# RWKV-7 layer on one Trainium2 core: squares for the norms summed on GpSimd, per-head sums issued in fours, low-rank second products on 128 rows

## The chip, the cores and the metric

The kernel runs on one core of one Trainium2 chip. A core has TensorE (PE, the matrix engine, which reads its stationary operand into the array and streams the other one through), VectorE (DVE), ScalarE (ACT), GpSimd (POOL) and SyncE (SP, which here only issues transfers). Each engine works through its own list of instructions in order; a semaphore makes one wait for another. The metric is the device time of one execution in microseconds, as the median of several runs.

## The reference

One layer (DEPTH is 1) on 2048 tokens of width 1024 in fp32, and a final norm:

```python
h = x
hn = rms_norm(h, norm_mix_g[i])
h = h + rwkv7_time_mix(hn, ...)
h = h + sq_relu_mlp(rms_norm(h, norm_ffn_g[i]), mlp_up[i], mlp_down[i])
return rms_norm(h, final_g)
```

Inside the time mix, what this case touches is

```python
w_log = -softplus(-(w0 + tanh(xw @ w1) @ w2)) - 0.5
a  = sigmoid(a0 + (xa @ a1) @ a2)            # w1, a1: 1024 x 64; w2, a2: 64 x 1024
kk = heads(k * k_k); kk = kk / max(norm(kk, axis=-1), 1e-12)
bonus = sum(r_h * k_h * r_k, axis=-1) * v_h  # 16 heads of 64
```

together with a recurrence over the tokens, a gate, and the output product. The MLP is `relu(x @ up)**2 @ down` with 4096 hidden columns.

## The kernel before, in words

Everything lies with the model's width on the partitions and tokens along the row: a tensor of a block is eight tiles of 128 rows by 512 tokens, and there are four blocks (NB). A product of fp32 operands is done on float32r tiles: each operand is split into a high part (a cast on ACT, L84 and L97) and the rest (a subtraction on DVE, L85 and L98), and `mm3` issues three matmuls of 512 columns (L90, L91, L92). Weights come by DMA (`wload`), 256 KB at a time.

**Phase A**, to about 690 us, does the projections of a block: `head(i)` loads the tokens and normalises them (norms a0 to a3), `lora(i)` does the first halves of the low-rank products, then `k_proj`, `r_proj` and `v_proj`. Beside the projections of a block runs `epilogue(i)` of the block before it, emitted in pieces after each eighth of `r_proj(i)` and `k_proj(i+1)`: reciprocal norms of the keys of each head, the second low-rank products into `pz` and `pq` (L388 and L389, L397 and L398), the decays, and what the recurrence reads (`ar`, `bk`), which goes to DRAM by DMAs issued on POOL's queue (L435, L436). `head(i+1)` and `lora(i+1)` are emitted within `r_proj(i)`.

**The low-rank second product.** `TW` holds the high part of `tanh(xw @ w1)` in rows 0 to 63 and the rest of it in rows 64 to 127; the weight's high part is loaded twice, in both halves of the rows. So L388 with 128 rows gives high times high plus high times rest. L389 adds the weight's low part times the high part of `TW`, with 64 rows. L397 and L398 do the same for `TA`, whose high part is in rows 64 to 127.

**Sums over a head.** In `k_proj` the square of each of the eight key tiles (`sq`, on ACT) is multiplied by a matrix with 32 columns (`selk`) into a strip of 32 rows of `psN`; tile m goes to strip m mod 4, and the two passes over the strips add up (L360). In `epilogue` the product `rk` = r times r_k times k (DVE, L431) goes the same way into `psO` (L433). One such matmul has 128 rows, 32 columns and 512 tokens, and each is issued when its row of data is ready. There are 8 in each of the 8 sums. In the trace a matmul of this kind, being fp32, leaves two records.

**norm(h)** (L105 to L127) is called 12 times: a0 to a3 in phase A, n0 to n3 before the MLP and f0 to f3 at the end of each block. ACT squares a tile (L110), and a matmul with 32 columns of ones (L112) adds up its partitions into strip k mod 4 of `pss`, again eight times. ACT copies `pss` out (L115); four matmuls with one column each (L118) sum the partitions once more into a column for each token (the ones are 1/32 there, because every strip holds 32 equal rows); DVE and ACT make the reciprocal root (L120 to L122), and four matmuls (L125) spread it over the 128 partitions. What follows waits for that: the normalised tiles of the next stage, or the output.

**Phase B** (about 690 to 1100 us) is the recurrence of the first block with products of other blocks as fillers. **Phase C** (to the end) does for each block the output product `c_out`, the norm `c_norm` (n), the MLP in groups (`c_up`, `c_down`) and the last norm `c_final` (f), with the recurrence of the next block in between. The order of the program is: last group of `c_down` first half, `c_out(i+1)`, `c_norm(i+1)`, `c_down` second half, `c_final(i)`, `c_up` of block i+1. `c_norm` keeps its spread reciprocal in a tile of the tag "rb", which has one buffer, and `c_final` takes the same buffer.

**The order of the work** on each engine is set when the program is built: a scheduler works from the emitted instructions, their dependences and buffers, and writes a fixed list for each engine. So an instruction may stand earlier or later than the place at which it was emitted.

**POOL** has almost nothing to compute: in phases B and C one select for each window (L574, 96 rows of 1024), and the issue of transfers (L293, L435, L436, L821).

Of the kernel before, what the change touches and what calls it, by code (L numbers as in the profile page):

```python
# [39 lines left out]
def trunk(ctx: ExitStack, tc, xt, vecs, lnw, lnb, wr, wk, wv, w1a1, w2, a2,  # L40
# [47 lines left out]
    def mm3(out, lhs, rhs, first, last):  # L88
        """out += lhs^T rhs for operands given as (high, low) pairs."""
        nc.tensor.matmul(out, lhs[0], rhs[0], start=first, stop=False)  # L90
        nc.tensor.matmul(out, lhs[0], rhs[1], start=False, stop=False)  # L91
        nc.tensor.matmul(out, lhs[1], rhs[0], start=False, stop=last)  # L92
# [12 lines left out]
    def norm(h, name, sb, ps, tag, tb, nb=1):  # L105
        """Reciprocal root mean square of each column of h, on all partitions."""
        pss = ps.tile([P, TB], F32, tag=tag, name=f"{name}s", bufs=nb)
        for k in range(KT):
            sq = sb.tile([P, TB], F32, tag="t0", name=f"{name}q{k}", bufs=tb)
            nc.scalar.activation(sq, h[k], AF.Square)  # L110
            j = k % 4
            nc.tensor.matmul(pss[32 * j:32 * j + 32], ones32[:, 0:32], sq, start=(k < 4), stop=(k >= 4),  # L112
                             skip_group_check=True, tile_position=(0, 32 * j))
        s = sb.tile([P, TB], F32, tag="t0", name=f"{name}c", bufs=tb)
        nc.scalar.copy(s, pss)  # L115
# [820 lines left out]
```

## Time and profile before

| what | value |
|---|---|
| median of three runs | 3051.98 us (3050.55 to 3055.19) |
| span of the profiled execution | 3052.7 us |
| PE busy | 2921.5 us, 96% of the span |
| DVE busy | 2029.8 us, 66% |
| ACT busy | 1450.6 us, 48% |
| POOL busy | 199.9 us, 7% |
| instructions | 50234 |

The profiled execution is 0.7 us longer than the median. Busy time is the time in which an engine had at least one instruction in work. A matmul of 512 columns shows about 0.39 us, but the next one begins 0.227 us after it, since matmuls overlap in the array: so what a matmul costs is read from the distance of the starts, and not from its duration. A view of windows gives, for a stretch of time, the busy time of each engine with its count of records. A view of groups gives, after the shape and the count, the busy time and the mean of one in nanoseconds, and after the bar the idle time before them and what ended it.

### The profile page before, as it was taken

What the parts mean: (1) busy time and instruction counts of PE and PEld (TensorE: products, weight loads), DVE (VectorE), ACT (ScalarE), POOL (GpSimd) and SP (SyncE); (2) the same over time, 40 slices, a digit from 0 to 9 for tenths busy, and PEclk for the clock granted to TensorE, in tenths of its full rate; (3) what the DMA queues carried; (4) which work ended last, traced back from release to release, by engine and by line L of the source; (5) the groups of instructions that cost most, each with busy time, mean ns of one, the idle gap of its engine ahead of it and who ended that gap; (6) DMA issues with size and microseconds to landing.
All of it is one profiled execution on the core that took longest, in us unless ns stands there. A gap on an engine that the chain in (4) does not pass through costs nothing.

```text
span 3052.7 us, 50234 instructions
## 1 busy us (share of the span) xinstructions
PE 2921.5 (96%) x19304; PEld 2126.9 (70%) x19304; DVE 2029.8 (66%) x3858; ACT 1450.6 (48%) x2649; POOL 199.9 (7%) x278
## 2 busy tenths in 40 slices
PE   7999999997899999999999999999999999999998
PEld 4756565655455577777776777777777777778886
DVE  4576767794788577676667678765866786454443
ACT  4556666663356344444444444443445435343442
POOL 0000000013021100000000000000000000000000
PEclk9999999998899999999999999999999999999999
DMA  3434444346564423333252333334233232332332
GB/s 120 147 135 154 146 155 146 130 172 214 162 179 160 155 88 112 113 97 111 89 159 87 108 94 111 112 100 150 90 111 107 92 117 87 104 118 94 96 100 76
DMA packets 192544, 373.94 MB, mean 122 GB/s; under 512 B 41136, under 2 KB 41712, under 8 KB 187696
## 3 DMA queue, kind: packets, MB, share of 16 engines
q1 hardware_dynamic: 175216, 305.49, 32.9%
q0 software_dynamic: 17088, 65.24, 5.5%
q8 instruction: 152, 2.49, 0.3%
q14 instruction: 88, 0.72, 0.1%
HBM read 303.32 MB, written 67.32 MB: 121 GB/s over the span
## 4 chain that ended last, share of the span: by engine, by line
PE 74%; DVE 13%; DMA 4%; ACT 4%; issue 3%; POOL 0%; SPq 0%; DVEq 0%; ACTq 0%; POOLq 0%
PE pd L92 7%; PE pd L90 6%; PE pd L91 6%; PE pu L90 6%; PE pu L91 6%; PE pu L92 6%; PE pv L176 2%; DVE tmp L580 2%; DVE M L581 2%; PE pr L92 2%; PE pr L90 2%; PE pk L90 2%; PE pk L91 2%; PE pr L91 2%; PE pk L92 2%
## 5 line engine op out<-in xcount | busy, mean ns | idle before, releaser
L92 PE MATMUL pd<-uh,d_wl 128*128 128x512 f32 x1024 | 408.7, 399 | 5.5 <-DVE d_wl L85 5.2
L90 PE MATMUL pd<-uh,d_wh 128*128 128x512 f32 x1024 | 407.3, 398 | 0.0
L91 PE MATMUL pd<-ul,d_wh 128*128 128x512 f32 x1024 | 404.3, 395 | 0.0
L84 ACT CAST d_wh<-d_w 128x512 fp32r<-128x512 f32 x256 | 158.5, 621 | 354.2 <-PE pu L91 157.9
L84 ACT CAST u_wh<-u_w 128x512 fp32r<-128x512 f32 x256 | 158.0, 621 | 312.1 <-PE pd L91 114.1
L812 DVE TENSOR_TENSOR h<-h,pd 128x512 f32<-128x512 f32 x256 | 174.2, 682 | 169.0 <-PE pd L92 168.2
L85 DVE TENSOR_TENSOR d_wl<-d_w,d_wh 128x512 fp32r<-128x512 f32 x256 | 180.6, 709 | 120.1 <-ACT d_wh L84 110.2
L85 DVE TENSOR_TENSOR u_wl<-u_w,u_wh 128x512 fp32r<-128x512 f32 x256 | 175.9, 693 | 90.1 <-ACT u_wh L84 73.1
L92 PEld LDWEIGHTS pd<-uh,d_wl 128*128 128x128 f32 x1024 | 193.0, 189 | 59.4 <-DVE d_wl L85 15.8
L91 PEld LDWEIGHTS pd<-ul,d_wh 128*128 128x128 f32 x1024 | 193.3, 189 | 46.6 <-issue 4.2
L90 PEld LDWEIGHTS pd<-uh,d_wh 128*128 128x128 f32 x1024 | 193.6, 189 | 44.2 <-issue 4.2
L580 DVE TENSOR_TENSOR tmp<-M 96x30 f32<-96x30 f32 (+14 forms) x480 | 156.2, 325 | 18.6 <-POOL M L574 8.1
L581 DVE TENSOR_TENSOR M<-M,tmp 96x30 f32<-96x30 f32 (+14 forms) x480 | 156.5, 326 | 11.1
L801 DVE TENSOR_TENSOR ul<-rl,uh 128x512 fp32r<-128x512 f32 x128 | 87.9, 687 | 65.8 <-ACT uh L800 65.6
L176 PE MATMUL pv<-v,xv 128*128 128x512 f32 x256 | 125.2, 625 | 5.9 <-DMA v<-in_wv 5.6
L562 PEld LDWEIGHTS sc<-Le,Bk 128*64 128x64 f32 x1024 | 66.3, 139 | 46.6 <-issue 33.2
L562 PE MATMUL sc<-Le,Bk 128*64 128x64 f32 x1024 | 76.9, 227 | 15.0 <-DMA Le<-d_ar 5.3
L634 PEld LDWEIGHTS pS<-suv,ls 128*64 128x64 f32 x1024 | 65.1, 137 | 34.4 <-ACT suv L631 26.5
L627 PEld LDWEIGHTS pu<-ws,xbd 128*128 128x128 f32 x512 | 65.1, 193 | 30.7 <-ACT xbd L594 16.5
L797 ACT ACTIVATE rl<-rl 128x512 f32<-128x512 f32 x128 | 80.9, 632 | 3.7
L634 PE MATMUL pS<-suv,ls 128*64 128x64 f32 x1024 | 75.0, 225 | 7.4 <-ACT suv L631 6.1
L627 PE MATMUL pu<-ws,xbd 128*128 128x64 f32 x512 | 67.5, 275 | 15.3 <-ACT xbd L594 9.2
(704 smaller groups left out, 7174.1 us busy)
## 6 DMA issues: line engine op xcount, KB each, us to landing
u_w<-in_up SPq DMA_DIRECT2D x256, 256.0 KB, 2.7
d_w<-in_down SPq DMA_DIRECT2D x256, 256.0 KB, 2.6
k_w<-in_wk SPq DMA_DIRECT2D x64, 256.0 KB, 2.6
r_w<-in_wr SPq DMA_DIRECT2D x64, 256.0 KB, 2.7
d_ar<-ar POOLq DMA_DIRECT2D x32, 512.0 KB, 3.2
d_bk<-bk POOLq DMA_DIRECT2D x32, 512.0 KB, 3.2
Bk<-d_bk SPq DMA_DIRECT2D x16, 1024.0 KB, 4.9
o_w<-in_wo SPq DMA_DIRECT2D x64, 256.0 KB, 2.9
```

The lines of the kernel that those rows point to most:

```text
L84: nc.scalar.copy(hi[0:rows, 0:cols], raw[0:rows, 0:cols])
L85: nc.vector.tensor_tensor(lo[0:rows, 0:cols], raw[0:rows, 0:cols], hi[0:rows, 0:cols], ALU.subtract)
L90: nc.tensor.matmul(out, lhs[0], rhs[0], start=first, stop=False)
L91: nc.tensor.matmul(out, lhs[0], rhs[1], start=False, stop=False)
L92: nc.tensor.matmul(out, lhs[1], rhs[0], start=False, stop=last)
L176: nc.tensor.matmul(pv[tt], xs_[k][:, c], w, start=(k == 0), stop=(k == KT - 1))
L562: nc.tensor.matmul(sc[64:128, p, :], bk[:, p, c, :], Le[:, p, c, :], start=(p == 0), stop=True, skip_group_check=True)
L580: nc.vector.tensor_tensor(tv, M[0:96, s + 1:32, s:s + 1].to_broadcast((96, n, s)), M[0:96, s:s + 1, 0:s].to_broadcast((96, n, s)), ALU.mult)
L581: nc.vector.tensor_tensor(M[0:96, s + 1:32, 0:s], M[0:96, s + 1:32, 0:s], tv, ALU.add)
L627: nc.tensor.matmul(pu[:, k, :], xbd[:, k, c, :], ws[:, k, :], start=(k == 0), stop=True, skip_group_check=True)
L634: nc.tensor.matmul(pS[0:64, p, :], lsc[0][:, p, :], S[0][:, p, :], start=(p == 0), stop=True, skip_group_check=True)
L812: nc.vector.tensor_add(h[m], h[m], pd)
```

## The change

The change has three parts. Comments are taken out as well, so line numbers move.

1. `norm` sums the squares on GpSimd. ACT's first square goes into a tile `s`, and each of the seven others is added to it by a GpSimd `tensor_tensor` (L124 of the changed kernel). The four matmuls that sum the partitions (L128 there) now read `s` and a column of 1.0. The matmuls of L112 and the copy of L115 go for ten of the twelve norms; with `late=True` (a0 and f3) the old way stays. `s` has one buffer: the tag "rb" in phase C, so the same as the spread reciprocals of `c_norm` and `c_final`, and "nsum" in phase A.
2. `headsum` issues the four matmuls of four tiles together, after the fourth; `sq` gets four buffers instead of two, and `rk` is written over `rr[m]`.
3. The second low-rank products take all 128 rows of the weight's low part (L405 and L414 there). This also adds the product of the low part and the rest.

```diff
+    def norm(h, name, sb, ps, tag, tb, nb=1, late=False, stag="rb"):
+        s = sb.tile([P, TB], F32, tag=stag, name=f"{name}c", bufs=1)
+        if late:
+            pss = ps.tile([P, TB], F32, tag=tag, name=f"{name}s", bufs=nb)
...
+            nc.scalar.copy(s, pss)
+            one = ones32[:, 32:33]
+        else:
+            nc.scalar.activation(s, h[0], AF.Square)
+            for k in range(1, KT):
+                sq = sb.tile([P, TB], F32, tag="t0", name=f"{name}q{k}", bufs=tb)
+                nc.scalar.activation(sq, h[k], AF.Square)
+                nc.gpsimd.tensor_tensor(s, s, sq, ALU.add)
+            one = ones32[:, 0:1]
...
-        psB = norm(xs, f"a{i}", am, psm, "mm", e.tb, e.mm)
+        psB = norm(xs, f"a{i}", am, psm, "mm", e.tb, e.mm, i == 0, "nsum")
...
+    def headsum(ps_, rows, half_):
+        for j in range(4):
+            nc.tensor.matmul(ps_[32 * j:32 * j + 32], selk[:, half_, :], rows[4 * half_ + j], start=(half_ == 0), stop=(half_ == 1),
+                             skip_group_check=True, tile_position=(0, 32 * j))
...
-            sq = ae.tile([P, TB], F32, tag="sq", name=f"sq{i}_{m}", bufs=2)
-            nc.scalar.activation(sq, pm, AF.Square, scale=vec[:, V_KK, m:m + 1])
-            j = m % 4
-            nc.tensor.matmul(psN[32 * j:32 * j + 32], selk[:, m // 4, :], sq, start=(m < 4), stop=(m >= 4),
+            sqs.append(ae.tile([P, TB], F32, tag="sq", name=f"sq{i}_{m}", bufs=4))
+            nc.scalar.activation(sqs[m], pm, AF.Square, scale=vec[:, V_KK, m:m + 1])
+            if m % 4 == 3:
+                headsum(psN, sqs, m // 4)
...
-                nc.tensor.matmul(pz, w2p[1][0:64, c], TW[0:64], start=False, stop=True)
+                nc.tensor.matmul(pz, w2p[1][:, c], TW, start=False, stop=True)
...
-                nc.tensor.matmul(pq, a2p[1][64:128, c], TA[64:128], start=False, stop=True)
+                nc.tensor.matmul(pq, a2p[1][:, c], TA, start=False, stop=True)
...
-                rk = ae.tile([P, TB], F32, tag="km", name=f"rk{i}_{m}", bufs=2)
-                nc.vector.scalar_tensor_tensor(rk, rr[m], vec[:, V_RK, m:m + 1], km, ALU.mult, ALU.mult)
-                j = m % 4
-                nc.tensor.matmul(psO[32 * j:32 * j + 32], selk[:, m // 4, :], rk, start=(m < 4), stop=(m >= 4),
+                nc.vector.scalar_tensor_tensor(rr[m], rr[m], vec[:, V_RK, m:m + 1], km, ALU.mult, ALU.mult)
+                if mm == 3:
+                    headsum(psO, rr, hf)
...
-        pb = norm(h, f"f{i}", cp, psb, "y0", 2)
+        pb = norm(h, f"f{i}", cp, psb, "y0", 2, 1, i == NB - 1)
```

What stands where on the engines, at three places. The names are those of the tiles (output, then inputs), with the number of the tile behind.

**PE behind the last output product of block 3 (norm n3), before.** `po3_7` is the last tile of that product, `n3q` are the squares, `pd2_7_4` is the first product of the second half of `c_down`.

```order
L92 MATMUL po3_7_24850<-z3_7h_24571,o3_7_1_wl_24872 128x512
L112 MATMUL n3s_24889<-n3q0_24890,ones32_100 32x512
L112 MATMUL n3s_24889<-n3q1_24893,ones32_100 32x512
L90 MATMUL pd2_7_4_25004<-uh2_28_23832,d2_7_0_1_wh_24982 128x512
L91 MATMUL pd2_7_4_25004<-ul2_28_23833,d2_7_0_1_wh_24982 128x512
L92 MATMUL pd2_7_4_25004<-uh2_28_23832,d2_7_0_1_wl_24983 128x512
L90 MATMUL pd2_7_4_25004<-uh2_29_24227,d2_7_1_1_wh_24988 128x512
L112 MATMUL n3s_24889<-n3q2_24896,ones32_100 32x512
L91 MATMUL pd2_7_4_25004<-ul2_29_24228,d2_7_1_1_wh_24988 128x512
L92 MATMUL pd2_7_4_25004<-uh2_29_24227,d2_7_1_1_wl_24989 128x512
L112 MATMUL n3s_24889<-n3q3_24899,ones32_100 32x512
L90 MATMUL pd2_7_4_25004<-uh2_30_24389,d2_7_2_1_wh_24994 128x512
```

And the same place in the changed kernel, where `n3c` is the sum that GpSimd makes:

```order
L92 MATMUL po3_7_24786<-z3_7h_24507,o3_7_1_wl_24808 128x512
L90 MATMUL pd2_7_4_24936<-uh2_28_23768,d2_7_0_1_wh_24914 128x512
L91 MATMUL pd2_7_4_24936<-ul2_28_23769,d2_7_0_1_wh_24914 128x512
L92 MATMUL pd2_7_4_24936<-uh2_28_23768,d2_7_0_1_wl_24915 128x512
L90 MATMUL pd2_7_4_24936<-uh2_29_24163,d2_7_1_1_wh_24920 128x512
L91 MATMUL pd2_7_4_24936<-ul2_29_24164,d2_7_1_1_wh_24920 128x512
L92 MATMUL pd2_7_4_24936<-uh2_29_24163,d2_7_1_1_wl_24921 128x512
L90 MATMUL pd2_7_4_24936<-uh2_30_24325,d2_7_2_1_wh_24926 128x512
L91 MATMUL pd2_7_4_24936<-ul2_30_24326,d2_7_2_1_wh_24926 128x512
L92 MATMUL pd2_7_4_24936<-uh2_30_24325,d2_7_2_1_wl_24927 128x512
L128 MATMUL n3t_24848<-ones32_100,n3c_24825 128x1 x4
L90 MATMUL pd2_7_4_24936<-uh2_31_24395,d2_7_3_1_wh_24932 128x512
```

The six places with L112 matmuls between the products are gone (two, one and one of them show above), and the four one-column matmuls that need the whole sum stand nine matmuls behind the last output product.

**PE in `k_proj` of block 2, changed kernel.** `sq2_0` to `sq2_3` are the four squares that are issued together; `pn1_5` belongs to the epilogue of block 1, `pk2_4` is the next tile of keys.

```order
L92 MATMUL pk2_3_3193<-xk2_7h_2980,k2_3_1_wl_3215 128x512
L354 MATMUL psN2_2927<-sq2_0_3023,selk_131 32x512
L354 MATMUL psN2_2927<-sq2_1_3064,selk_131 32x512
L354 MATMUL psN2_2927<-sq2_2_3168,selk_131 32x512
L425 MATMUL pn1_5_3243<-nh1_2383,selb_137 128x512
L426 MATMUL pn1_5_3243<-nl1_2384,selb_137 128x512
L90 MATMUL pk2_4_3261<-xk2_0h_2931,k2_4_0_wh_3264 128x512
L354 MATMUL psN2_2927<-sq2_3_3232,selk_131 32x512
L91 MATMUL pk2_4_3261<-xk2_0l_2932,k2_4_0_wh_3264 128x512
```

Three of the four stand side by side and the fourth alone, three matmuls later. All sixteen fours were counted in this way over the whole list: the eight of `psN` stand as three and one; of `psO`, in blocks 0 to 2 one stands as one and three and the other as four; in block 3 they are split into seven places. So 64 places with such matmuls become 16 + 9 + 7 = 32.

**PE and ACT at the last norm of block 0 (f0).** Before, PE has, behind the first tile of `c_up(1)`:

```order
L112 MATMUL f0s_14677<-f0q6_14696,ones32_100 32x512
L92 MATMUL pu1_1_14803<-hn1_1h_14464,u1_1_0_wl_14807 128x512
L90 MATMUL pu1_1_14803<-hn1_2h_14470,u1_1_0_wh_14806 128x512
L112 MATMUL f0s_14677<-f0q7_14699,ones32_100 32x512
L91 MATMUL pu1_1_14803<-hn1_2l_14471,u1_1_0_wh_14806 128x512
L92 MATMUL pu1_1_14803<-hn1_2h_14470,u1_1_0_wl_14807 128x512
```

In the changed kernel ACT has the squares (`f0c` is the first one, `f0q1` the second) behind the last cast of the normalised tiles of block 1, `hn1_7h`, and PE has the one-column matmuls `f0t` here:

```order
L90 MATMUL pu1_0_14680<-hn1_5h_14436,u1_0_1_wh_14701 128x512
L91 MATMUL pu1_0_14680<-hn1_5l_14437,u1_0_1_wh_14701 128x512
L92 MATMUL pu1_0_14680<-hn1_5h_14436,u1_0_1_wl_14702 128x512
L90 MATMUL pu1_0_14680<-hn1_6h_14442,u1_0_1_wh_14701 128x512
L91 MATMUL pu1_0_14680<-hn1_6l_14443,u1_0_1_wh_14701 128x512
L92 MATMUL pu1_0_14680<-hn1_6h_14442,u1_0_1_wl_14702 128x512
L90 MATMUL pu1_0_14680<-hn1_7h_14448,u1_0_1_wh_14701 128x512
L128 MATMUL f0t_14648<-ones32_100,f0c_14625 128x1 x4
L91 MATMUL pu1_0_14680<-hn1_7l_14449,u1_0_1_wh_14701 128x512
```

So `f0t` moved from the second tile of `c_up(1)` to the end of its first tile, one matmul behind the first use of the cast after which the squares begin. For f1 it stands six matmuls ahead of the first use of `hn2_7h`, and for f2 eighteen matmuls behind `hn3_7l`.

More of the change, by code (lines that the diff above doesn't have):

```diff
@@ L103, in trunk @@
     nc.vector.memset(ones32[:, 32:33], 1.0 / 32.0)
[L105 to L115, printed above, removed]
+    def norm(h, name, sb, ps, tag, tb, nb=1, late=False, stag="rb"):
+        s = sb.tile([P, TB], F32, tag=stag, name=f"{name}c", bufs=1)
+        if late:
+            pss = ps.tile([P, TB], F32, tag=tag, name=f"{name}s", bufs=nb)
+            for k in range(KT):
+                sq = sb.tile([P, TB], F32, tag="t0", name=f"{name}q{k}", bufs=tb)
+                nc.scalar.activation(sq, h[k], AF.Square)
+                j = k % 4
+                nc.tensor.matmul(pss[32 * j:32 * j + 32], ones32[:, 0:32], sq, start=(k < 4), stop=(k >= 4),
+                                 skip_group_check=True, tile_position=(0, 32 * j))
[4 more added lines that the diff above has]
+            for k in range(1, KT):
+                sq = sb.tile([P, TB], F32, tag="t0", name=f"{name}q{k}", bufs=tb)
+                nc.scalar.activation(sq, h[k], AF.Square)
+                nc.gpsimd.tensor_tensor(s, s, sq, ALU.add)
+            one = ones32[:, 0:1]
         pt = ps.tile([P, NWB], F32, tag=tag, name=f"{name}t", bufs=nb)
         for tt in range(NWB):
-            nc.tensor.matmul(pt[:, tt:tt + 1], s[:, tt * P:tt * P + P], ones32[:, 32:33], start=(tt == 0), stop=True, skip_group_check=True)
+            nc.tensor.matmul(pt[:, tt:tt + 1], s[:, tt * P:tt * P + P], one, start=(tt == 0), stop=True, skip_group_check=True)
         rs = sb.tile([P, NWB], F32, tag="rs", name=f"{name}r", bufs=2)
@@ L339, in r_proj @@
             yield
+    def headsum(ps_, rows, half_):
+        for j in range(4):
+            nc.tensor.matmul(ps_[32 * j:32 * j + 32], selk[:, half_, :], rows[4 * half_ + j], start=(half_ == 0), stop=(half_ == 1),
+                             skip_group_check=True, tile_position=(0, 32 * j))
     def k_proj(i, start=None):
@@ L344, in k_proj @@
         rks[i] = [[], kr, psN]
+        sqs = []
         xs_ = mixed(e, (lambda k: (next(start), hn[:, k, :])[1]) if start else hn_of, V_MK, f"xk{i}")
@@ L356, in k_proj @@
             nc.scalar.copy(kr[m], pm)
-            sq = ae.tile([P, TB], F32, tag="sq", name=f"sq{i}_{m}", bufs=2)
-            nc.scalar.activation(sq, pm, AF.Square, scale=vec[:, V_KK, m:m + 1])
-            j = m % 4
-            nc.tensor.matmul(psN[32 * j:32 * j + 32], selk[:, m // 4, :], sq, start=(m < 4), stop=(m >= 4),
-                             skip_group_check=True, tile_position=(0, 32 * j))
+            sqs.append(ae.tile([P, TB], F32, tag="sq", name=f"sq{i}_{m}", bufs=4))
+            nc.scalar.activation(sqs[m], pm, AF.Square, scale=vec[:, V_KK, m:m + 1])
+            if m % 4 == 3:
+                headsum(psN, sqs, m // 4)
             yield
@@ L429, in epilogue @@
                 nc.vector.tensor_mul(bk[:, :, :, CH:64], v4(km), eiv)
-                rk = ae.tile([P, TB], F32, tag="km", name=f"rk{i}_{m}", bufs=2)
-                nc.vector.scalar_tensor_tensor(rk, rr[m], vec[:, V_RK, m:m + 1], km, ALU.mult, ALU.mult)
-                j = m % 4
-                nc.tensor.matmul(psO[32 * j:32 * j + 32], selk[:, m // 4, :], rk, start=(m < 4), stop=(m >= 4),
-                                 skip_group_check=True, tile_position=(0, 32 * j))
+                nc.vector.scalar_tensor_tensor(rr[m], rr[m], vec[:, V_RK, m:m + 1], km, ALU.mult, ALU.mult)
+                if mm == 3:
+                    headsum(psO, rr, hf)
                 nc.gpsimd.dma_start(d_ar[i][:, :, m].rearrange("w p c z -> p w (c z)"), ar.rearrange("p w c z -> p w (c z)"))
```

## Prediction

> **What bounds the kernel now.** I read the page first: its span, the busy times and the chain of waits.
>
> ```profile
> span 3052.7 us, 50234 instructions
> PE 2921.5 (96%) x19304; PEld 2126.9 (70%) x19304; DVE 2029.8 (66%) x3858; ACT 1450.6 (48%) x2649; POOL 199.9 (7%) x278
> PE 74%; DVE 13%; DMA 4%; ACT 4%; issue 3%; POOL 0%; SPq 0%; DVEq 0%; ACTq 0%; POOLq 0%
> ```
>
> PE is busy in 96% of the span and makes up 74% of the chain that ended last; DVE is second, GpSimd nowhere. What a microsecond off PE is worth depends on the stage, so I read the windows view next (columns: window, its length, then the busy time and records of PE, PEld, DVE, ACT and POOL, and the clock): two stretches of block 1 in phase A, the end of phase A, and a stretch of phase C.
>
> ```profile
> 310.00:360.00 50.00, 47.25 (x156) 25.03 (x155) 43.59 (x88) 30.02 (x51) 6.57 (x9) 0.97 0.48 174
> 370.00:440.00 70.00, 70.00 (x263) 44.47 (x262) 49.76 (x86) 44.80 (x80) 7.13 (x10) 1.00 0.39 136
> 600.00:690.00 90.00, 82.80 (x308) 53.94 (x307) 81.61 (x144) 60.33 (x104) 12.60 (x17) 1.00 0.49 170
> 2700.00:3000.00 300.00, 300.00 (x1317) 246.85 (x1316) 131.74 (x196) 114.24 (x190) 0.35 (x1) 1.00 0.32 101
> ```
>
> In phase C PE never stops and DVE works 44% of the time, so PE time taken away there is worth its full amount. 1317 matmuls in 300 us are 0.228 us each, and I use 0.227, the step in the rows below. At 310 to 360 and 600 to 690, DVE is busy 87% and 91%: there PE time is worth only what DVE's slack lets through.
>
> **What the removed matmuls cost.** A busy time hides this, since matmuls overlap; the timeline of PE (start, duration) shows the starts.
>
> ```profile
> 412.73 0.39 PE L91 MATMUL pk<-xk_1l,k_wh 128*128 128x512 f32 x1
> 413.05 1.05 PE L360 MATMUL psN<-sq,selk 128*32 128x512 f32 x2
> 414.02 0.50 PE L92 MATMUL pk<-xk_1h,k_wl 128*128 128x512 f32 x1
> 414.36 0.39 PE L90 MATMUL pk<-xk_2h,k_wh 128*128 128x512 f32 x1
> ...
> 2649.69 0.39 PE L92 MATMUL po<-z_7h,o_wl 128*128 128x512 f32 x1
> 2650.01 1.05 PE L112 MATMUL n3s<-n3q,ones 128*32 128x512 f32 x4
> 2650.99 0.51 PE L90 MATMUL pd<-uh,d_wh 128*128 128x512 f32 x1
> 2651.33 0.40 PE L91 MATMUL pd<-ul,d_wh 128*128 128x512 f32 x1
> ...
> 860.46 1.92 PE L189 MATMUL pt<-xg,g1t 128*32 128x512 f32 x16
> 862.31 1.12 PE L199 MATMUL pg<-xg,g 128*128 128x512 f32 x2
> ```
>
> With one 32-column matmul in between, 412.73 to 414.36 is 1.63 us for two ordinary steps (0.45): it costs 1.18. Two side by side (x4 records) cost the same, 2651.33 − 2649.69 − 0.45 = 1.19. Eight in a row (x16) take 1.85. So the cost is that of the interruption and hardly of the number: I take 1.18 for a cluster of one to four.
>
> The low-rank second product (L389, 64 rows) and its neighbours:
>
> ```profile
> 397.98 0.39 PE L91 MATMUL pk<-xk_7l,k_wh 128*128 128x512 f32 x1
> 398.20 0.39 PE L388 MATMUL pz<-TW,w_wh 128*128 128x512 f32 x1
> 398.52 0.49 PE L389 MATMUL pz<-TW,w_wl 64*128 64x512 f32 x1
> 398.94 0.50 PE L92 MATMUL pk<-xk_7h,k_wl 128*128 128x512 f32 x1
> 399.28 0.40 PE L409 MATMUL pn<-nh,selb 128*128 128x512 f32 x1
> ```
>
> Four matmuls take 1.30 us instead of 4 × 0.227 = 0.91: the 64-row one costs 0.39 more than one of 128 rows such as L388. The changed one should step like L388; if it is not the rows that make it late, the gain is 0.
>
> Counts and the gross gain on PE:
>
> ```profile
> L360 PE MATMUL psN<-sq,selk 128*32 128x512 f32 x64 | 33.9, 612 | 4.7 <-ACT sq L358 4.5
> L112 PE MATMUL n0s<-n0q,ones 128*32 128x512 f32 x16 | 5.7, 604 | 1.1 <-ACT n0q L110 1.0
> L112 PE MATMUL a3s<-a3q,ones 128*32 128x512 f32 x16 | 4.7, 605 | 0.3 <-ACT a3q L110 0.3
> ```
>
> - Norms: n1 to n3 and f0 to f2 lose six clusters each, 6 × 6 × 1.18 = 42.5. n0 is not between products, so its own busy time counts, 5.7; a1 to a3 count 4.7 each by the row of a3, 14.1.
> - Head sums: x64 records are 32 matmuls in `psN`, and as many in `psO`. The order of the changed kernel has 32 places instead of 64: 32 × 1.18 = 37.8.
> - Low rank: 64 products × 0.39 = 25.0.
>
> Gross 125 us: 48 in phase C, 77 in phase A.
>
> **The work that takes their place.** Seventy GpSimd adds, 128x512 with two inputs. The trace has none; the nearest row is the select on POOL (one input), and what DVE does beside it:
>
> ```profile
> L574 POOL TENSOR_SCALAR_AFFINE_SELECT M<-M x16: 1260/1570/2297, 760.8 to 2490.9; 96x1024 f32<-96x1024 f32 x16
> ...
> 2270.52 1.56 POOL L574 TENSOR_SCALAR_AFFINE_SELECT M<-M 96x1024 f32<-96x1024 f32 x1 [22.41 <-DVE M L573]
> ...
> 2270.32 0.63 DVE L812 TENSOR_TENSOR h<-h,pd 128x512 f32<-128x512 f32 x1
> 2270.88 1.73 DVE L85 TENSOR_TENSOR d_wl<-d_w,d_wh 128x512 fp32r<-128x512 f32 x1
> 2272.66 0.67 DVE L85 TENSOR_TENSOR d_wl<-d_w,d_wh 128x512 fp32r<-128x512 f32 x1
> ```
>
> 1024 columns take 1.26 us at least, so 512 take 0.63: the lower bound for an add. Twice the inputs give at most 1.26. And beside the select the subtraction L85, with both inputs in SBUF, takes 1.73 instead of 0.67, while L812, with one input in PSUM, is not held up. So an add can also wait for one such DVE operation: upper bound 1.26 + 0.67 = 1.93. I take 1.1, since part of the 0.63 is a fixed cost that does not double. A sum of seven then is ready 1.26 (two squares) + 7 × 1.1 = 9.0 us after the first square starts.
>
> By the Trainium skill (GPSIMD Engine Reference, 3.1 Elementwise — side-by-side cycle accounting) an add of 2048 fp32 columns takes 4497 ns on GpSimd against 2293 on DVE, an estimate of 1.12 us for 512, and the page keeps elementwise work for DVE; no run here shows it yet, and by it the sum below would stay within 1 us. The Trainium skill (SBUF — State Buffer, SBUF: two separate sides) has DVE with two SBUF inputs and GpSimd take a shared pair of ports as an exclusive lock; the trace agrees (1.73 beside 0.67), and the rule's result is the slower rival below.
>
> *n1 to n3.* Only the last add is late, as the other seven squares come with their tiles. After the last output product: the residual add on DVE, a square, an add.
>
> ```profile
> 2650.11 0.69 DVE L772 TENSOR_TENSOR h<-po,h 128x512 f32<-128x512 f32 x1 [1.60 <-PE po L92]
> ```
>
> It ends at 2650.80; with 0.63 for the square and 1.1 for the add the sum is there at 2652.6, 2.9 us after the last product began, while PE has nine products, 2.0 us, ahead of `n3t`. With handing over, 1.2 us of waiting each, 3.6 in all. For n0 I count no wait: PE waits for its squares already (1.1 in its row).
>
> *f0 to f2.* Here the squares cannot begin before the casts of the next block's tiles, because the sum lies in the buffer "rb" that these tiles are still made from. All eight squares and seven adds then follow in one go. f0 (ACT's last cast, and what PE did around it):
>
> ```profile
> 1633.38 0.62 ACT L97 CAST hn_7h<-hn 128x512 fp32r<-128x512 f32 x1
> ...
> 1634.09 0.23 PE L621 MATMUL pw<-suv,Le 128*32 128x64 f32 x2
> 1636.49 0.27 PE L562 MATMUL sc<-Le,Bk 128*64 128x64 f32 x1
> 1637.58 1.05 PE L112 MATMUL f0s<-f0q,ones 128*32 128x512 f32 x4
> ...
> 2675.68 0.62 ACT L97 CAST hn_7h<-hn 128x512 fp32r<-128x512 f32 x1
> 2676.30 0.50 PE L92 MATMUL pu<-hn_4h,u_wl 128*128 128x512 f32 x1 [2.03 <-DVE u_wl L85]
> ```
>
> The cast ends at 1634.0, the sum at 1643.0. PE is through with `pw` at 1634.3, has the sixteen `sc` (1636.49 to 1637.58, 1.1) and eight products (1.8), and stands at `f0t` from 1637.1: it waits 6.0. f1t stands seven products earlier (1.6): 7.6. For f2 the sum is ready at 2676.30 + 9.0 = 2685.3; PE, at 2676.30 on `hn_4h`, has 27 products to `f2t` with that one, 6.1, and comes at 2682.4: 2.9. Behind `f0t` all of PE's list waits. Together 16.5 us, a new price of the change.
>
> Phase C: 48.2 − 3.6 − 16.5 = **28**.
>
> **Phase A.** `k_proj(0)` has PE to itself: four places fewer, 4.7. Blocks 0 to 2 each have two stretches. In the one like 370 to 440 go four places of `psN`, three of `psO` and half the low-rank products: 7 × 1.18 + 8 × 0.39 = 11.4. PE is the bound, and DVE would have 49.8 of 58.6: I count 9, as it will be the later one now and then. In the one like 310 to 360 go a norm, two places and eight low-rank products: 4.7 + 2.4 + 3.1 = 10.2. But DVE has 43.6 us of work in 50, none of which goes, and the seven adds fall here and hold up its operations: by half an add each, 3.9. Of 6.4 us of slack 2.5 to 3 are left: 3. The last block loses one place and its low-rank products, 7.4, against 8.4 us of slack on DVE in short pieces: 2. Phase A: 4.7 + 3 × (9 + 3) + 2 = **43**.
>
> GpSimd's queue: in phase A the adds stand among the issues of `ar` and `bk`, and one that waits for a late DVE product holds up the adds behind it; I have no row for that and leave it in the range. In phase C only selects and, after f, the output's transfers stand there. The copy L115 goes from ACT, which has slack everywhere (44.8 of 70). Writing `rk` over `rr[m]` costs DVE the same operation; `rr` is next written a block later.
>
> Sum: 28 + 43 = 71 us, 3052.7 − 71 = 2981.7, and the median is 0.7 below the profiled execution: **2981**.
>
> **Rivals.**
> - *Nearly all of it arrives* (2936). If an add takes 0.65, the chain is 1.26 + 4.55 = 5.8, f0 to f2 wait 2.8, 4.4 and 0, the n's 0.75 each: phase C gives 48.2 − 9.5 = 38.7. If DVE in phase A follows PE, 77 more: 116. For it: DVE's 66%; its operations stand in the way only where PE waits for them. Against: 43.6 of 50.
> - *Little arrives* (3018). Adds at 1.93 make a chain of 14.8 us: f0 to f2 wait 11.8, 13.4 and 8.7, the n's 2.0 each, and phase C gives 8. In phase A the adds take DVE's whole slack in the first stretch, the second keeps 7, the last block 0: 4.7 + 21 = 26. Together 34.
> - *Slower* (3062). GpSimd's adds and DVE's two-input operations shut each other out at every norm, and PE waits at `n3t`, `f0t` and the like for the whole sum, or for the weights that DVE could not split meanwhile. Then each add is on PE's path. It decides from 125 / 70 = 1.78 us for an add; at 1.93 it is 135 − 125 = 10 us lost. For it: 1.73 beside 0.67. Against: the squares of n0 to n3 come with their tiles, so six of their seven adds lie beside PE's products, and DVE's 44% at 2700 to 3000 leaves room.
> - *The fours do not do what they say* (3008): a matmul waits for the one before, also in another strip, and a three costs 3 × 1.18. Then the head sums' part, about 27 of the 43, stays away. Against: two at one price, eight in 1.85.
>
> **How the numbers follow.** Forecast 0.55, nearly all 0.18, little 0.20, fours 0.04, slower 0.03. The likeliest gives 2981; the range goes from 2935, below the second, to 3020, above the third. 0.2%, 6 us, is what a measurement can tell: only the last case is slower, 0.03; 0.03 more for a sum of bad ends within 0.2%; faster 0.94.
>
> **What would show it.** The adds (L124) at 0.63 to 1.93 us, and DVE's L85 beside them above 1.1. PE idle at `f0t` and `f1t` of about 6 and 8 us, released by POOL, and 1 us at `n3t`. A place with three or four L354 costing 1.2 by the starts around it, and L405 stepping 0.227. Phase A shorter by some 43 us, with a higher share of DVE. I am wrong if phase A keeps its length, if the f's wait 12 us or more, or if L405 still costs 0.6.

## The result and the profile after

The changed kernel takes 2982.75 us (median of 4 runs, 2978.28 to 2985.68), the kernel before 3051.27 us (4 runs): a ratio of 0.977, interval 0.9756 to 0.9784. The forecast was 2981, within 2935 to 3020. The total is right; its two large terms are not, they err in opposite directions, and that the sum still fits to 2 us is luck.

The page of the changed kernel, its span, the busy times and the chain:

```profile
span 2976.6 us, 50052 instructions
PE 2819.1 (95%) x19144; PEld 2129.0 (72%) x19144; DVE 2050.7 (69%) x3858; ACT 1440.7 (48%) x2639; POOL 297.5 (10%) x348
PE 67%; DVE 15%; issue 6%; ACT 5%; DMA 5%; POOL 2%; SPq 0%; ACTq 0%; DVEq 0%; POOLq 0%
```

GpSimd went from 200 to 298 us, and from 0 to 2% of the chain. VectorE is 21 us busier although it has exactly as many instructions (x3858): some of them now last longer. The profiled execution is the quickest of the four, 2978.28 us, 73.0 below the median of the kernel before in this comparison, where the medians differ by 68.5.

The new waits of PE, grouped by the one-column matmuls that need a whole sum (after the bar: idle time before them, and what ended it):

```profile
L128 PE MATMUL n0t<-ones,n0c 128*128 128x1 f32 x8 | 1.9, 355 | 8.6 <-POOL n0c L124 8.6
L128 PE MATMUL f0t<-ones,f0c 128*128 128x1 f32 x8 | 1.9, 355 | 5.8 <-POOL f0c L124 5.8
L128 PE MATMUL f1t<-ones,f1c 128*128 128x1 f32 x8 | 1.9, 354 | 6.0 <-POOL f1c L124 6.0
L128 PE MATMUL f2t<-ones,f2c 128*128 128x1 f32 x8 | 1.9, 355 | 5.6 <-POOL f2c L124 5.6
L128 PE MATMUL n1t<-ones,n1c 128*128 128x1 f32 x8 | 1.1, 253 | 0.7 <-POOL n1c L124 0.7
L128 PE MATMUL a3t<-ones,a3c 128*128 128x1 f32 x8 | 1.1, 253 | 1.0 <-POOL a3c L124 1.0
```

The rows with a long wait show a second thing: the matmuls themselves took 355 ns instead of 253. The windows view around f0t tells why (the last three columns are the granted clock, the DMA share and GB/s):

```profile
1570.00:1575.00 5.00, 2.65 (x29) 1.89 (x24) 3.62 (x3) 1.85 (x5) 4.76 (x4) 1.00 0.44 134
1575.00:1580.00 5.00, 1.51 (x7) 1.51 (x8) 1.38 (x2) 1.46 (x4) 3.28 (x3) 0.53 0.06 24
1580.00:1585.00 5.00, 5.00 (x13) 4.00 (x14) 3.45 (x7) 2.75 (x6) 2.29 (x1) 0.50 0.16 41
1585.00:1590.00 5.00, 5.00 (x26) 4.30 (x25) 4.21 (x8) 1.98 (x4) 1.64 (x3) 0.95 0.50 171
```

During the wait the granted clock falls to half, and it comes back only at about 1585.5. From the end of the wait (1578.5) until then, 7 us, PE is busy but does half the work, so the wait of 5.8 us at f0t costs some 3.5 us more behind it. At f1 and f2 the slow stretch behind the wait is shorter, 5.4 and 4.8 us, and costs about half of that.

Where the time went, from the starts of the same matmuls in the timelines of both profiled executions (in us): at the first product of `v_proj(0)` the changed kernel is 11.0 ahead, at the first recurrence matmul (end of phase A) 61.3, at the first output product 61.4, at the end 76.1. So phase A gave 61 where 43 was forecast, phase B nothing, phase C 15 where 28 was forecast. By the medians the whole gain is 68.5, so this execution shows some 8 us more than the usual one.

### The profile page after: what moved, and what is told of

Read it like the earlier page. It is cut to its first block, busy times and chain, and to the rows that moved or that the text cites. A ratio compares the mean times of both kernels' runs of the same rounds, so it can differ in the third digit from the quotient of the medians.

```text
span 2976.6 us, 50052 instructions
## 1 busy us (share of the span) xinstructions
PE 2819.1 (95%) x19144; PEld 2129.0 (72%) x19144; DVE 2050.7 (69%) x3858; ACT 1440.7 (48%) x2639; POOL 297.5 (10%) x348
## 4 chain that ended last, share of the span: by engine, by line
PE 67%; DVE 15%; issue 6%; ACT 5%; DMA 5%; POOL 2%; SPq 0%; ACTq 0%; DVEq 0%; POOLq 0%
PE pd L92 6%; PE pd L91 6%; PE pd L90 6%; PE pu L91 6%; PE pu L90 6%; PE pu L92 5%; DVE tmp L595 2%; DVE M L596 2%; PE pk L90 2%; PE pk L91 2%; PE pk L92 2%; PE po L90 2%; PE po L92 2%; PE po L91 2%; PE pr L90 2%
## 5 line engine op out<-in xcount | busy, mean ns | idle before, releaser
L92 PE MATMUL pd<-uh,d_wl 128*128 128x512 f32 x1024 | 407.2, 398 | 5.9 <-DVE d_wl L85 5.7
L85 DVE TENSOR_TENSOR d_wl<-d_w,d_wh 128x512 fp32r<-128x512 f32 x256 | 179.2, 703 | 120.9 <-ACT d_wh L84 110.7
L85 DVE TENSOR_TENSOR u_wl<-u_w,u_wh 128x512 fp32r<-128x512 f32 x256 | 179.2, 705 | 88.7 <-ACT u_wh L84 78.8
L92 PEld LDWEIGHTS pd<-uh,d_wl 128*128 128x128 f32 x1024 | 192.4, 188 | 56.7 <-DVE d_wl L85 14.9
L596 DVE TENSOR_TENSOR M<-M,tmp 96x30 f32<-96x30 f32 (+14 forms) x480 | 158.3, 330 | 11.2
L577 PE MATMUL sc<-Le,Bk 128*64 128x64 f32 x1024 | 77.5, 228 | 17.4 <-DVE Lo L581 7.4
L566 POOL MEMSET Le<- 64x2048 f32 x16 | 28.9, 1804 | 610.5 <-PE y L672 551.5
L811 ACT ACTIVATE rl<-pu 128x512 f32<-128x512 f32 x128 | 76.0, 594 | 23.2 <-PE pu L92 20.3
L642 PE MATMUL pu<-ws,xbd 128*128 128x64 f32 x512 | 67.7, 275 | 16.2 <-ACT xbd L609 8.3
```

Of the source, the lines that this page charges most:

```text
L85: nc.vector.tensor_tensor(lo[0:rows, 0:cols], raw[0:rows, 0:cols], hi[0:rows, 0:cols], ALU.subtract)
L577: nc.tensor.matmul(sc[64:128, p, :], bk[:, p, c, :], Le[:, p, c, :], start=(p == 0), stop=True, skip_group_check=True)
L596: nc.vector.tensor_tensor(M[0:96, s + 1:32, 0:s], M[0:96, s + 1:32, 0:s], tv, ALU.add)
L642: nc.tensor.matmul(pu[:, k, :], xbd[:, k, c, :], ws[:, k, :], start=(k == 0), stop=True, skip_group_check=True)
```

## The experiments

Each kernel was compared with the kernel before on the same chip; differences of medians are against that. Profiled executions of kernels with the same phase A differ by some microseconds there: in six kernels that share it, it was 55 to 61 us shorter than before. So differences of a few microseconds between two such kernels are not read.

**The three parts alone.** The fours alone: the kernel before with

```diff
+            sqs.append(ae.tile([P, TB], F32, tag="sq", name=f"sq{i}_{m}", bufs=4))
+            if m % 4 == 3:
+                headsum(psN, sqs, m // 4)
...
+                if mm == 3:
+                    headsum(psO, rr, hf)
```

> The kernel before with the fours alone (32 places with head-sum matmuls instead of 64), norms and low-rank products as before. Theory A (each place costs PE 1.18 us and phase A passes nearly all of it on, since the trace of the changed kernel shows phase A 61 us shorter): 32 x 1.18 = 38 us gross, and some 30 to 38 of it arrive: 3014 to 3021. Theory B (the prediction's: DVE binds half of phase A): about 27 us arrive: 3024. Theory C (the gain of phase A comes from the norms' sums): under 15 us, above 3036.

Measured: 3009.86 us against 3053.33, ratio 0.9859 (0.9839 to 0.988): 43 us, with an interval of 37 to 49, so nearly all of the 38 us gross arrive, or all. In `k_proj(0)` more than the gross price arrives, since a single also waited there. The first head sum of block 0 in the timeline of the kernel before:

```profile
41.08 0.62 ACT L84 CAST k_wh<-k_w 128x512 fp32r<-128x512 f32 x1 [7.23 <-DMA k_w<-in_wk]
...
42.08 0.69 ACT L358 ACTIVATE sq<-pk,vec 128x512 f32<-128x512 f32 x1
42.91 1.52 PE L360 MATMUL psN<-sq,selk 128*32 128x512 f32 x2 [4.00 <-ACT sq L358]
```

the windows view of the same kernel there,

```profile
43.00:48.00 5.00, 5.00 (x8) 1.77 (x8) 0.00 (x0) 0.00 (x0) 0.00 (x0) 0.66 0.50 161
```

and the same stretch with the fours (the rows of the windows view, 43 to 48 us):

```profile
43.00:48.00 5.00, 5.00 (x21) 3.62 (x20) 1.14 (x2) 3.64 (x6) 0.00 (x0) 1.00 0.48 154
```

PE waited 4.0 us for ACT's square, and went on at a clock of 0.66. The square was late because ACT, which works in order, had stood for 7.23 us at a cast whose weights DMA had yet to bring. With the fours that cast is hardly earlier (40.53), but PE now has other products ahead of the sum: it does not wait, and at `v_proj(0)` this kernel is 11.7 us ahead, where four places fewer explain 4.7. Theory A.

The wide low-rank products alone (the kernel before with `w2p[1][:, c], TW` and `a2p[1][:, c], TA`):

> The kernel before with the second low-rank products on all 128 rows alone. Theory A (64 x 0.39 = 25 us on PE, nearly all passed on): 18 to 25 us, 3026 to 3033. Theory B (half of these products stand where DVE binds): about 11 us, 3040. The product itself steps 0.227 in both.

Measured: 3037.93, ratio 0.9948 (0.9933 to 0.9963): 15 us of 25 gross, between the theories. The product itself is repaired for the most part, as the timeline of the changed kernel shows:

```profile
365.25 0.39 PE L92 MATMUL pk<-xk_6h,k_wl 128*128 128x512 f32 x1
365.49 0.50 PE L404 MATMUL pz<-TW,w_wh 128*128 128x512 f32 x1
365.83 0.40 PE L405 MATMUL pz<-TW,w_wl 128*128 128x512 f32 x1
366.06 0.40 PE L90 MATMUL pk<-xk_7h,k_wh 128*128 128x512 f32 x1
366.30 0.40 PE L91 MATMUL pk<-xk_7l,k_wh 128*128 128x512 f32 x1
```

L405 is followed after 0.23 us, but L404 only after 0.34. The four steps from L92 on take 1.05 us where the prediction's rows had 1.30, so 0.25 goes and not 0.39. Over all 64 products the medians are 0.28 (`pz`) and 0.31 (`pq`), so the gross gain in the changed kernel is about 19 us and not 25. By the starts of the projections, 8 us arrive in `k_proj(1)` to `k_proj(3)` and 5.5 in the last block, but only 3 in `r_proj(0)` to `r_proj(2)`, which have as many of these products as the three `k_proj`.

The norms on GpSimd alone (the kernel before with the new `norm` and its calls):

> The kernel before with the sums of the norms on GpSimd alone. Theory A: in phase C n1 to n3 give some 6 us each, n0 loses about 4 and each f loses about 3 (wait of 5.8 us and half the clock for some 8 us behind it, against 7.1 saved), so about 5 us there, and 10 in phase A: 3035 to 3040. Theory B (the prediction's sum): phase C gives 28 and phase A 5: 3018. If the adds held DVE up more than the matmuls cost: above 3051.

Measured: 3043.79, ratio 0.9966 (0.9953 to 0.9979): 10 us of 62 gross. In the profiles 1 us of it lies in phase A, the rest in phase C. The three parts alone sum to 68 us, and together they give as much: they hardly touch each other, and the norms, the first part of the change, give the least.

**Is it the wait at f0 to f2?** All f's on PE as before (`norm(..., True)` in `c_final`), the rest as changed:

> The changed kernel with f0 to f2 summed on PE as before; a1 to a3 and n0 to n3 stay on GpSimd. Theory A (a wait of 5.8 us for GpSimd's sum and the half clock behind it cost more than the 7.1 us that six clusters cost): some 5 us less than the changed kernel, 2977, and the stretch from the last output product of a block to the fourth tile of the MLP is 6 us shorter than in the kernel before, in all three blocks. Theory B (the f's still bring their share, the missing part is lost at n1 to n3): 2985 or more.

Measured: 2974.56 against 3048.87, ratio 0.9753 (0.9738 to 0.9769), against 0.977 (0.9756 to 0.9784) of the changed kernel. By the medians of the differences 74.3 and 68.5, some 6 us better, as theory A has it; the intervals overlap. The stage says it more clearly. The table gives, for each block, the change of the stretch from the last output product (before n) to the eighth product of the MLP (behind f of the block before), against the kernel before; gross would be −14 for n and f together, −6 for n0 alone.

| kernel | n0 | n1, f0 | n2, f1 | n3, f2 |
|---|---|---|---|---|
| changed | +5.1 | −3.9 | −2.7 | −7.4 |
| f0 to f2 on PE | +5.7 | −10.0 | −5.2 | −7.9 |
| f in two pieces | +4.9 | −6.8 | −2.6 | −8.7 |
| f in three pieces | +5.4 | −8.1 | −4.3 | −8.4 |
| three pieces, n0 on PE | +2.2 | −6.4 | −5.4 | −9.1 |
| own buffer for f's sum | +7.1 | −3.4 | −2.5 | −7.4 |
| adds on VectorE | +0.8 | −10.9 | −7.6 | −15.6 |
| norms alone, GpSimd | +6.2 | −4.5 | −1.4 | −6.0 |
| norms alone, VectorE | +0.8 | −9.1 | −7.4 | −15.6 |

Putting f0 and f1 back on PE gains 6 and 2.5 us, f2 half a microsecond. On GpSimd none of the f's was worth anything.

**Can the wait be moved away?** In two pieces, the squares and adds (up to the yield) stay, and `f0t` and all behind it is emitted after the third `c_up` of the next block, 48 products later:

```diff
     def c_final(i):
-        pb = norm(h, f"f{i}", cp, psb, "y0", 2, 1, i == NB - 1)
+        g = norm_steps(h, f"f{i}", cp, psb, "y0", 2, 1, i == NB - 1)
+        next(g)
+        yield
+        pb = next(g)
```

> The changed kernel; the squares and adds of f0 to f2 stay where they are, but the rest of the norm (the one-column matmuls f0t and on) is emitted behind the third product of the next block's MLP, 48 matmuls (11 us) later on PE. Theory A: the waits of 5.8, 6.0 and 5.6 us go, and with them the stretch of half clock behind each (some 4 us): about 30 us less than the changed kernel, 2953. Theory B (the slow stretch has another cause, only the wait goes): 17 us less, 2965. Theory C (the chain of adds holds up the splitting of weights, and PE waits elsewhere): less than 5 us, above 2977.

Measured: 2980.1 against 3053.33, ratio 0.9758 (0.974 to 0.9776): by the medians of the differences 5 us better than the changed kernel (73.2 and 68.5), with intervals that overlap: theory C. No wait is left at f0t, but two of the places with the longest waits of PE are now

```profile
PE f1b L136 <- ACT f1r L133: 4.2, 1, 4.2
PE f0b L136 <- ACT f0r L133: 3.7, 1, 3.7
```

VectorE's two steps ahead of the root stand behind its triangular solve of the recurrence, and five products after `f0t` the spreading matmuls want the root. In three pieces, with room at both places (`f0t` behind the third product, `f0b` behind the fourth):

> The changed kernel with the norms of f0 to f2 emitted in three pieces: squares and adds where they are, the one-column matmuls behind the third product of the next block's MLP, the spreading matmuls (f0b and on) behind the fourth. In the run with two pieces PE waited 3.7 and 4.2 us at f0b and f1b for the root, which stood behind VectorE's triangular solve. Theory A (each wait is only a place where PE comes too early, and each is followed by slow matmuls): with room at both places every f gives its 7 us: 20 to 25 us less than the changed kernel, 2958 to 2963. Theory B (the work itself, adds and VectorE, is the limit, and PE waits at a third place): 2975 or more.

Measured: 2978.82 against 3048.87, ratio 0.9769 (0.9736 to 0.9802): no better, theory B, though not because of the adds. Up to the fourth product the stretches are 13.2 and 11.3 us shorter than before, the full gain; the next four give 5 and 7 us back. The waits of PE in that stretch of this kernel, and VectorE's timeline there:

```profile
PE pd L92 <- DVE d_wl L85: 3.8, 1, 3.8
```

```profile
1610.37 0.74 DVE L845 SCALAR_TENSOR_TENSOR h<-h,vec,fB 128x512 f32<-128x512 f32 x1
...
1612.22 0.68 DVE L85 TENSOR_TENSOR d_wl<-d_w,d_wh 128x512 fp32r<-128x512 f32 x1
```

The eight multiplications of `c_final` (L845; the last is shown) now stand directly ahead of the splitting of the weights for `c_down`, and PE waits there. The wait was moved twice, and each time it met VectorE's next dependent piece.

The same with n0 on PE (`norm(..., i == 0)` in `c_norm`):

> As the run with three pieces, and n0 summed on PE as before. Theory A (seven adds hold VectorE's solve up for about 1 us each, so the residual add and with it n0's sum come 6 us late, and PE waits 8.6 us): 5 us less than with three pieces, 2953 to 2958; n0's stretch is as long as in the kernel before. Theory B (n0's late sum comes from the earlier phases, which PE went through faster than VectorE): no difference, PE waits as long for the squares.

Measured: 2970.76, ratio 0.9739 (0.9722 to 0.9756): 8 us better than with three pieces by the medians, with intervals that overlap, and 3 by n0's own stretch (+5.4 to +2.2). Theory A for the cause, though only a part of its 5 us arrives at n0. In the kernel before, the last residual add ends 3.2 us after the last output product of block 0 began:

```profile
1109.16 0.39 PE L92 MATMUL po<-z_7h,o_wl 128*128 128x512 f32 x1
1111.66 0.68 DVE L772 TENSOR_TENSOR h<-po,h 128x512 f32<-128x512 f32 x1
```

GpSimd and VectorE at n0 in the changed kernel:

```profile
1048.78 1.46 POOL L124 TENSOR_TENSOR n0c<-n0c,n0q 128x512 f32<-128x512 f32 x1 [4.82 <-ACT n0q L123]
1055.53 1.30 POOL L124 TENSOR_TENSOR n0c<-n0c,n0q 128x512 f32<-128x512 f32 x1 [5.29 <-ACT n0q L123]
...
1049.15 1.33 DVE L596 TENSOR_TENSOR M<-M,tmp 96x220 f32<-96x220 f32 x1
1050.52 0.38 DVE L595 TENSOR_TENSOR tmp<-M 96x210 f32<-96x210 f32 x1
1053.99 0.68 DVE L787 TENSOR_TENSOR h<-po,h 128x512 f32<-128x512 f32 x1
1055.75 1.24 DVE L595 TENSOR_TENSOR tmp<-M 96x130 f32<-96x130 f32 x1
```

Beside an add the solve's step takes 1.33 and 1.24 us instead of 0.38 and 0.3. VectorE is the engine that decides here: its last residual add (L787) ends at 1054.7, 7.2 us after the last output product began (1047.4), and the last square and add come behind it. With n0 on PE the stretch is still 2 us longer than before, which stays open.

**Was it the buffer?** The prediction says that the squares of f cannot begin earlier because the sum lies in "rb". A buffer of its own (and one `rl` less, for room, which is a second difference):

```diff
-        pb = norm(h, f"f{i}", cp, psb, "y0", 2, 1, i == NB - 1)
+        pb = norm(h, f"f{i}", cp, psb, "y0", 2, 1, i == NB - 1, "fs")
```

> The changed kernel with a buffer of its own for the sum of the f's (and, to make room, one buffer instead of two for the squared-ReLU tile rl). Theory A (the prediction's step: the squares of f stand behind the next block's casts because the sum lies in the buffer rb): the squares come earlier, f0t waits less than 3 us, 2965. Theory B (the other seven squares go through the ring t0 of two buffers, which the next block's normalised tiles use just before, so they stay behind hn_7h, and only the first one moves): the waits stay between 5 and 6 us, 2980 to 2986.

Measured: 2987.98 against 3051.89, ratio 0.9788 (0.9774 to 0.9803), and the waits are as before:

```profile
L128 PE MATMUL f0t<-ones,f0c 128*128 128x1 f32 x8 | 1.9, 355 | 6.4 <-POOL f0c L124 6.4
L128 PE MATMUL f1t<-ones,f1c 128*128 128x1 f32 x8 | 1.9, 355 | 6.0 <-POOL f1c L124 6.0
```

Theory B: "rb" held up the first square only, which now begins at 1500.9 for f0; the other seven go through the ring "t0" and begin from 1575.6 on, behind the next block's last cast (over at 1575.1). Freeing both was not run.

**Was it GpSimd?** One word changed, in the changed kernel:

```diff
-                nc.gpsimd.tensor_tensor(s, s, sq, ALU.add)
+                nc.vector.tensor_tensor(s, s, sq, ALU.add)
```

> The changed kernel with the 70 adds on VectorE instead of GpSimd. Theory A (an add on GpSimd takes 1.29 us and holds one two-input operation of VectorE up for about 1 us, while VectorE's own add takes 0.7): the f's wait 2 us or less instead of 5.8, n0's wait of 8.6 us becomes 6 or less: 2960 to 2970. Theory B (VectorE has no room; GpSimd's work is free beside it): phase A and the solves of the recurrence get longer by the 49 us of adds in part, above 2990.

Measured: 2952.41 against 3048.87, ratio 0.9681 (0.9654 to 0.9707): some 28 us better than the changed kernel, and the fastest kernel here. Theory A, beyond its numbers. The groups of adds and the waits:

```profile
L124 DVE TENSOR_TENSOR n0c<-n0c,n0q 128x512 f32<-128x512 f32 x7 | 4.8, 684 | 0.1
L124 DVE TENSOR_TENSOR f0c<-f0c,f0q 128x512 f32<-128x512 f32 x7 | 4.7, 671 | 0.0
...
L128 PE MATMUL n0t<-ones,n0c 128*128 128x1 f32 x8 | 1.6, 322 | 0.1
L128 PE MATMUL f0t<-ones,f0c 128*128 128x1 f32 x8 | 0.9, 239 | 0.0
L128 PE MATMUL f1t<-ones,f1c 128*128 128x1 f32 x8 | 1.1, 253 | 0.9 <-DVE f1c L124 0.9
```

```profile
PE 2815.8 (95%) x19144; PEld 2126.2 (72%) x19144; DVE 2067.7 (70%) x3928; ACT 1440.7 (49%) x2639; POOL 202.6 (7%) x278
```

The waits are gone. And VectorE, with 70 more instructions of 0.68 us (48 us), is only 17 us busier than in the changed kernel: its other instructions add up to 2209 us there, 2186 here and 2193 in the kernel before, so GpSimd's adds had stretched them by some 20. The run changes two things at once, the time of an add (0.68 for 1.29 us) and the stretching, and does not part them.

The norms alone with adds on VectorE, against the norms alone on GpSimd:

> The kernel before with ten norms summed on VectorE instead of PE, and nothing else. With GpSimd's adds this part alone gave 10 us of 62 gross. Theory A (the part is right and only its engine is wrong): 35 to 45 us, 3006 to 3016. Theory B (VectorE's adds help only where the fours and the wide products have already freed it): 20 us or less, above 3030.

Measured: 3009.04 against 3051.89, ratio 0.9855 (0.9839 to 0.9872): 43 us instead of 10. Theory A. 12 of them lie in phase A, where on GpSimd it was 1, and where a1 to a3 are 14 gross.

All twelve norms with adds on VectorE:

> The changed kernel with the adds on VectorE, for all twelve norms, a0 and f3 too. Theory A: as the run with VectorE's adds (2952), and f3's clusters (5.7 us on PE) and its copy go at the very end, a0's last matmul and copy at the very start: 6 to 8 us less, 2945. Theory B (at both ends the norm is a chain of its own, in which an add takes the place of a matmul and a copy): the same time, 2952 within 3 us.

Measured: 2960.76, ratio 0.9701 (0.9681 to 0.972): not better than ten of them; theory B, or a little worse, with intervals that overlap. The trace shows both theories at work. At the end f3 does gain: from the last product of the MLP to the end it is 16.2 us instead of 20.2 in the run with ten. At the start as much is lost: at the first product of `v_proj(0)` this kernel is 4.0 us behind the run with ten, and PE waits there for weights (`wm`) that VectorE now prepares later, which it does not in the run with ten:

```profile
PE psL L320 <- DVE wm L317: 3.3, 1, 3.3
```

## Why the prediction was right, and where it was not

**Prices of what is removed: right for the head sums, too high for the low rank.** Three head-sum matmuls side by side cost what one did (timeline of the changed kernel):

```profile
374.06 0.39 PE L92 MATMUL pk<-xk_7h,k_wl 128*128 128x512 f32 x1
374.38 1.06 PE L354 MATMUL psN<-sq,selk 128*32 128x512 f32 x6
375.37 0.50 PE L425 MATMUL pn<-nh,selb 128*128 128x512 f32 x1
375.71 0.39 PE L426 MATMUL pn<-nl,selb 128*128 128x512 f32 x1
```

375.71 − 374.06 − 0.45 = 1.20, and the rival of the fours falls. Of the 0.39 of a 64-row product 0.28 to 0.31 is gone, so that term was a quarter too large.

**Phase A: 61 instead of 43.** The starts of the first product of each projection part the gain by stage. The stretch like 310 to 360 lies in `r_proj(1)`, the one like 370 to 440 in `k_proj(2)`. In us, from the profiled executions; gross and forecast are the prediction's:

| stage | gross | forecast | changed | fours alone | wide products alone | norms alone, GpSimd | norms alone, VectorE |
|---|---|---|---|---|---|---|---|
| start to `r_proj(0)` | 4.7 | 4.7 | 10.6 | 11.7 | 0.5 | 1.2 | −1.2 |
| `k_proj(1)` to `(3)` | 34.2 | 27 | 32.5 | 25.9 | 8.1 | 0.6 | 0.6 |
| `r_proj(0)` to `(2)` | 30.6 | 9 | 12.2 | 3.3 | 3.2 | −1.0 | 10.6 |
| last block | 7.4 | 2 | 6.0 | 3.5 | 5.5 | 0.5 | 1.9 |

Three terms were too small. `k_proj(0)` gave more than twice its price: I had the row L360 with 4.5 us of idle time for ACT's squares in the fence, priced the matmuls and not the wait, nor the slow clock behind it. In the other `k_proj` nearly all of the gross gain arrives, so the allowance for a late VectorE was not needed, and in the last block 6 of 7.4, where VectorE's slack was to leave 2. The fours alone gave 43 us where about 27 of the sum were theirs.

The term for the stretches like 310 to 360 came out about as priced, 12 for 9 (7 to 12 in the six kernels with this phase A), but its reason is not confirmed. With the norms alone and adds on VectorE, VectorE has 21 adds, 14 us, more to do in phase A, and 10.6 of the 14.1 us of a1 to a3 arrive all the same. On GpSimd nothing of them does. What the changed kernel loses in `r_proj(1)` is seen in the windows of that stage, before and after:

```profile
291.30:376.10 84.80, 80.82 (x291) 49.49 (x290) 62.52 (x117) 51.76 (x87) 6.57 (x9) 0.98 0.47 162
264.80:346.70 81.90, 75.01 (x277) 50.97 (x275) 66.62 (x115) 49.34 (x84) 16.27 (x16) 0.94 0.49 167
```

PE is idle for 6.9 us instead of 4.0, and the clock of 0.94 instead of 0.98 costs some 3 us more. Together that is most of the 7 us by which the stage (2.9 us shorter) falls short of its 10.2 gross. Which of the waits there would have to go was not run.

**Phase C: 15 instead of 28.** Of its terms:

- The add. 1.1 was taken, the groups show 1.26 to 1.30 undisturbed; "at most 1.26" from twice the one-input select was a shade low. With VectorE's split of weights in the way the adds of f0 come every 1.69 us at first, as the squares behind them show:

```profile
1566.64 0.63 ACT L120 ACTIVATE f0c<-h 128x512 f32<-128x512 f32 x1
1569.39 0.63 ACT L123 ACTIVATE f0q<-h 128x512 f32<-128x512 f32 x1 [0.84 <-POOL f0c L124]
1571.08 0.63 ACT L123 ACTIVATE f0q<-h 128x512 f32<-128x512 f32 x1 [1.05 <-POOL f0c L124]
1572.77 0.63 ACT L123 ACTIVATE f0q<-h 128x512 f32<-128x512 f32 x1 [1.06 <-POOL f0c L124]
```

  From the first square to f0t (1578.49) it is 11.9 us instead of 9.0.
- The waits of f0, f1, f2: 6.0, 7.6 and 2.9 forecast, 5.8, 6.0 and 5.6 measured, 17.4 in all for 16.5. The cause was half right: the ring of the squares holds them back as well as "rb". That f0 fits is luck: the sum came 2.9 us later than priced, and PE stood at `f0t` 5.9 us behind the cast instead of 3.1.
- What follows the wait, PE at half clock for 7.1, 5.4 and 4.8 us, was not in the sum. Half of these times, 8.6 us in all, is lost, which makes each f a loss or nothing.
- n0: 5.7 of gain counted and no wait; it lost 5. The step "PE waits for its squares already" overlooked that the squares come from VectorE's residual adds, and that seven adds on GpSimd lengthen VectorE's solve.
- n1 to n3: 1.2 forecast, 0.7 and 0.8 measured.

So 28 − 10.8 (n0) − 8.6 − 0.9 (the waits of f) + 1.4 (those of n) leaves 9, which is what the four stretches of the table in "Is it the wait at f0 to f2?" give together. The other 6 us of the 15 lie outside them. The kernel with the fours alone, whose norms are as before, also gains 7 us behind the first output product, which speaks against the norms as their cause; it stays open.

**The slower rival** named the right mechanism, GpSimd's adds and VectorE's two-input operations in each other's way, and the wrong size: not 135 us, but at most the difference between the two engines' kernels, some 28, which holds the longer add as well. That an operation with one input in PSUM is spared did not follow from the row of L812, which began before the select; the changed kernel shows it: `Le<-sc,mask`, with `sc` in PSUM, takes 0.69 us in the five cases that begin beside an add, and 0.69 otherwise.

The Trainium skill (SBUF — State Buffer, SBUF: two separate sides) calls GpSimd and VectorE's two-input operations exclusive of each other; the trace of the changed kernel agrees, 1.24 to 1.33 beside 0.3 to 0.38 above. The Trainium skill (GPSIMD Engine Reference, 3.1 Elementwise — side-by-side cycle accounting) also keeps elementwise sums for VectorE: 0.68 against 1.29 us here, and the kernel that follows it is 28 us faster.

## What to carry to other kernels

An engine that is idle is not free: before work goes to it, look for what it shares with the engine that the critical one waits for, and try the plain choice too; here the busier engine was the better place by 28 us. Price a removed instruction by the starts around it and by the wait in front of it, since a lone matmul that waits for its data stops all of PE. And a wait that is moved is only gone if the next dependent piece has room as well: look at what the engine behind it has to do next.

## What the runs showed of the hardware that was not expected

- PE pays for a wait twice. After 5.8 us at f0t the granted clock was 0.53 and 0.50 in two windows, and the ordinary step 0.43 instead of 0.227 us until about 1585.5 (7 us behind the end of the wait). With f0 on PE the clock is 1.00 throughout 1550 to 1600; with adds on VectorE it is at half for 3.4 us only (1570.4 to 1573.8), behind a wait of 1.8 us for weights. The Trainium skill (TensorE: Matmul & The Clock Gate, Part 1: The HAM clock gate) says that an idle window of about 3.4 us brings the clock to half, and a busy one of the same length brings it back; the trace agrees in kind but not in the length. In the changed kernel a wait of 2.2 us, over at 281, was enough for 3.4 us at half clock (281.7 to 285.1), while one of 2.2 us at 417 left the clock at 1.00. What decides between them was not measured here.
- One GpSimd add of 128x512 takes 1.26 to 1.30 us where nothing holds it up, and while it runs a VectorE operation with two inputs in SBUF that starts later stands still until it ends (L596 in the rows at n0): L85 of the weights r_wl went from a mean of 683 to 784 ns over 64.

```profile
L85 DVE TENSOR_TENSOR r_wl<-r_w,r_wh 128x512 fp32r<-128x512 f32 x64 | 49.6, 784 | 19.1 <-ACT r_wh L84 13.0 <-PE pn L426 6.1
```

- Three matmuls of 32 columns in different strips cost 1.20 us together, one costs 1.18.
